# Five more of layer 0's modulation pairs made by TensorE

## The chip, the cores and the metric

The kernel runs on one core of a Trainium2 chip. The metric is the device time of one execution in microseconds. The core has TensorE (matmuls and their weight loads), VectorE, ScalarE, GpSimd, and SyncE, whose queue issues most of the DMAs. Each engine works through its own instructions in order, and semaphores order the engines among each other.

## The reference, cut to what matters

A diffusion backbone of two layers over 256 latent and 256 context tokens, width 1024. Each layer's token and channel mixers are modulated by six vectors, which come from a conditioning vector and a large matrix:

```python
def adaln(cvec, w, b):
    mod = jax.nn.silu(cvec) @ w + b
    return jnp.split(mod[..., None, :], 6, axis=-1)

def modulate(xn, shift, scale):
    return xn * (1 + scale) + shift
...
    for i in range(DEPTH):
        sh1, sc1, g1, sh2, sc2, g2 = adaln(c, ada_w[i], ada_b[i])
        csh1, csc1, cg1, csh2, csc2, cg2 = adaln(c_ctx, ada_w[i], ada_b[i])
        a = modulate(rms_norm(h, norm_mix_g[i]), sh1, sc1)
        ...
        h = h + g1 * y
        a = modulate(rms_norm(h, norm_ffn_g[i]), sh2, sc2)
```

Layer 0 has a short gated convolution (an input projection to three blocks of 1024, a convolution over three tokens, an output projection) and a dense SwiGLU; layer 1 has differential attention and a top-2-of-8 expert SwiGLU. All in float32.

## The kernel before, in words

**Weights.** Matrix weights come in units of 128x2048 float32 (1 MB). `Loads` issues their DMAs on SyncE's queue (line 53) into three raw tiles `rw`. `Parts.pump` splits a unit in a high part (line 88, a cast on ScalarE) and a low part (line 92, a subtraction on VectorE), in three pairs of tiles. A product is three matmuls, high by high, high by low, low by high (`mm3`, lines 199 to 201); a unit holds 16 blocks of 128x128, so 48 matmuls. Splits and loads are issued when the one that holds the tile is through.

**Modulation.** `ada_w` of a layer comes as 24 pairs: pair u holds two blocks of 128 output columns (for u below 8 the shift and the scale of one block of 128 channels; 8 to 11 are the first gate, 12 to 19 shift and scale of the channel mixer, 20 to 23 the second gate). `ada` (line 272) makes a pair on VectorE: four passes of 128x1024, one for each block and stream (line 279, `junk<-ra,cb`), each with a sum over the row. `ada_pe` (line 285) makes a pair on TensorE: 16 fp32 matmuls with weights of 128x128 from the raw tile and two columns (line 292, `st<-cT,ra`), into a PSUM tile `st`. It is a generator: the first two steps issue the matmuls of one block each and the second of them frees the raw tile; the third issues the end operations. These (`ada_end`, bias at line 266, gain at line 270) run on VectorE in both cases. Before the change pairs 0, 1 and 3 go by `ada_pe`, whose weights lie in the raw tile with their rows in the partitions.

Raw pairs are loaded by `aloads`, on SyncE's queue too. After the first pairs, which have four more tiles `rx`, two tiles `ra` serve all pairs in turn: pair u+2 is loaded when pair u has been consumed (`aloads.done`).

**Order.** It is written out by hand. At the start of the mixer, `mod(k)` modulates block k of the tokens (VectorE and ScalarE, lines 338, 339, 334), and `main(k)` issues 18 matmuls with it, for the first six output tiles; `main(0)` to `main(7)` use units 0 to 2. Between them stand the pairs 2 to 7 and the splits of units 1 and 2. Then comes the loop over j = 2 to 7: three tiles of 24 matmuls each (`mm`), behind the first and the second tile one pair each (`ada(0, 8)` to `ada(0, 19)`), and `conv(j, ...)`, which ends in `uh[j]` and `ul[j]` (lines 500 to 510). Seven PSUM banks serve the tiles. The output projection takes 96 matmuls over all eight `uh`, `ul` (units 12, 13), and `last_tiles` the rest of it, in matmuls of 256 columns, with the sums of squares (line 315) for the next norm.

Of the kernel before, what the change touches and what calls it, by code (L numbers as in the profile page):

```python
# [20 lines left out]
P = 128  # L21
D = 1024
KT = D // P
# [5 lines left out]
U = 2048  # L29
B = U // P  # L30
GROUPS = (6, 8, 8)
ADA_PE = (0, 1, 3)
NE = 8
HV = (0,)
NCH = FT // 2
# [107 lines left out]
def backbone(ctx: ExitStack, tc: tile.TileContext, i, out):  # L143
# [277 lines left out]
    ms = []  # L421
    run = ada_pe(1)
# [21 lines left out]
    def mod(k):  # L444
        modulate([(k, s, rs[s], ms[k], ah[k], al[k]) for s in range(2)])

    def main(k, between=None):
        for n, f in enumerate(first):
            mm3(f, *next(w), ah[k], al[k], k == 0, k == KT - 1)
            if n == 2 and between is not None:  # L450
                between()
# [15 lines left out]
    ms += [next(run), m4]  # L467
    mod(3)
    main(2)
    mod(4)  # L470
    ms.append(ada(0, 5))
    mod(5)
# [2 lines left out]
    loads.limit = len(units)  # L475
    loads.advance()
    main(3)
    ms.append(ada(0, 6))
    mod(6)
    ms.append(ada(0, 7))  # L480
    mod(7)
# [8 lines left out]
    with tc.tile_pool(name="sc", bufs=1, reuse_waits="tile") as pc:  # L490
        yp = [pc.tile([P, 2, T + 2], F32, name=f"yp{n}") for n in range(2)]
        for y in yp:
            V.memset(y, 0.0)
        uh = [pc.tile([P, T2], F32R, name=f"uh{k}") for k in range(KT)]
        ul = [pc.tile([P, T2], F32R, name=f"ul{k}") for k in range(KT)]

        def conv(j, cg, xv, bg):
            y = yp[j % 2]
            c = tp.tile([P, T2], F32, name="cs")
            A.copy(c, cg)  # L500
            V.tensor_tensor(out=y[:, :, 1:T + 1], in0=xv.rearrange("p (s t) -> p s t", s=2),
                            in1=c.rearrange("p (s t) -> p s t", s=2), op=OP.mult)
            t = tp.tile([P, 2, T], F32, name="ct")
            A.activation(t, y[:, :, 0:T], AF.Identity, scale=convw[:, 0, j:j + 1])
            V.scalar_tensor_tensor(t, y[:, :, 1:T + 1], convw[:, 1, j:j + 1], t, op0=OP.mult, op1=OP.add)
            V.scalar_tensor_tensor(t, y[:, :, 2:T + 2], convw[:, 2, j:j + 1], t, op0=OP.mult, op1=OP.add)
            f = t.rearrange("p s t -> p (s t)")
            V.tensor_tensor(out=f, in0=bg, in1=f, op=OP.mult)
            A.copy(uh[j], f)
            V.tensor_tensor(out=ul[j], in0=f, in1=uh[j].bitcast(F32), op=OP.subtract)  # L510

        conv(0, *first[:3])
        conv(1, *first[3:])
        for j in range(2, KT):
            ps = [bank() for _ in range(3)]
            for n, f in enumerate(ps):
                mm(f, w, ah, al)
                if n < 2:
                    mod0.append(ada(0, 8 + len(mod0)))
            conv(j, *ps)  # L520

        ps = [bank() for _ in range(4)]
        for k in range(KT):
            for f in ps:
                mm3(f, *next(w), uh[k], ul[k], k == 0, k == KT - 1)
        accs = [Squares(), Squares()]
        for m, f in enumerate(ps):
            for s in range(2):
                gated(f[:, half(s)], m, mod0[m // 2], s)
                accs[s].put(X[s][m])  # L530

        def last_tiles(n, hi, lo, gates, acc, mods):

            parts.release()
            parts.holding = True
            ms = range(4, KT)
            ws = [[next(w) for k in range(n)] for m in ms]
            parts.pump()

            def norm(s):  # L540
                rs = rstd(mean(acc[s], st()), s)
                return [(k, s, rs, mods[k], ah[k], al[k]) for k in range(KT)]

            def add(f, m, s):
                gated(f[:, :T], m, gates[m // 2], s)
                acc[s].put(X[s][m])

            fs = []
            for s in range(2):
                for m, b in zip(ms, ws):  # L550
                    f = bank()
                    mm(f[:, :T], b, hi, lo, half(s))
                    fs.append((f, m, s))
                    if s == 0:
                        add(f, m, s)
                    elif m == 4:
                        jobs = norm(0)
                        modulate(jobs[:4])
                    elif m == 5:
                        for j in fs[-2:]:  # L560
                            add(*j)
                        modulate(jobs[4:])
                    elif m == KT - 1:
                        for j in fs[-2:]:
                            add(*j)
            acc[1].sum()
            parts.give(1)
            parts.release(0)
            parts.holding = True
            return lambda: norm(1)  # L570

        then = last_tiles(KT, uh, ul, mod0, accs, mod0[4:])
# [891 lines left out]
def lay_out(a):  # L1464
    a = {k: np.asarray(v) for k, v in a.items()}
    x = np.concatenate([a["x"][0], a["ctx"][0]], 0)
    r = {"xT": np.ascontiguousarray(x.T.reshape(KT, P, 2, T).transpose(2, 1, 0, 3))}
    r["cc"] = np.concatenate([a["c"][0], a["c_ctx"]])[None]
    r["cT"] = np.ascontiguousarray(r["cc"].reshape(2, KT, P).transpose(2, 1, 0))
    pair = [g * KT + k for k in range(KT) for g in (0, 1)]  # L1470
    order = pair + list(range(16, 24)) + [24 + p for p in pair] + list(range(40, 48))

    adaT = a["ada_w"].reshape(2, D, 48, P).transpose(0, 2, 3, 1)[:, order]
    r["ada"] = np.ascontiguousarray(adaT.reshape(2, 24, 2, P, D).transpose(0, 1, 3, 2, 4)).reshape(2, 24, P, U)
    for k in ADA_PE:
        w = a["ada_w"][0].reshape(KT, P, 48, P)[:, :, [k, KT + k]]
        r["ada"][0, k] = w.transpose(1, 0, 2, 3).reshape(P, U)
    r["ada_b"] = np.ascontiguousarray(a["ada_b"].reshape(2, 48, P)[:, order].transpose(2, 0, 1))
    g = np.stack([a["norm_mix_g"][0], a["norm_ffn_g"][0], a["norm_mix_g"][1], a["norm_ffn_g"][1]])
    r["gain"] = np.ascontiguousarray(g.reshape(4, KT, P).transpose(2, 0, 1))  # L1480
    r["conv"] = np.ascontiguousarray(a["sc_conv_w"][0].reshape(3, KT, P).transpose(2, 0, 1))
    si = _tiles(a["sc_in_w"][0]).reshape(3, KT, KT, P, P)[[1, 2, 0]]
    so = _tiles(a["sc_out_w"][0])
    bl = [si[:, :2].transpose(2, 1, 0, 3, 4).reshape(-1, P, P), si[:, 2:].transpose(1, 0, 2, 3, 4).reshape(-1, P, P),
          so[:4].transpose(1, 0, 2, 3).reshape(-1, P, P), so[4:].reshape(-1, P, P)]
    w13 = np.stack([_tiles(a["ffn_w1"][0]), _tiles(a["ffn_w3"][0])], 1)
    w2 = _tiles(a["ffn_w2"][0])
    f = 0
    for n in GROUPS:
        bl += [w13[f:f + n].reshape(-1, P, P), w2[:, f:f + n].reshape(-1, P, P)]  # L1490
        f += n
    r["w0"] = _units(np.concatenate(bl))
    w = a["da_qkv_w"][0].reshape(2, 4, P, 3, 4, T).transpose(4, 0, 2, 1, 3, 5)
    qkv = np.concatenate([w[:, :, :, :, :2].reshape(4, 2, P, U), w[:, :, :, :, 2].transpose(0, 2, 1, 3, 4).reshape(4, 1, P, U)], 1)
    qkv = qkv.reshape(12, P, U)
    do = a["da_out_w"][0].reshape(4, 2, P, D).transpose(0, 2, 1, 3).reshape(4, P, U)
    r["w1"] = np.concatenate([qkv, do])
    r["qkg"] = np.concatenate([a["da_q_norm_g"][0], a["da_k_norm_g"][0]])[None]
    r["subg"] = a["da_sub_norm_g"][0][:, None]
    r["lam"] = a["da_lambda"][0].reshape(1, 256)  # L1500
    pos = np.arange(T)
    inv = np.float32(10000.0) ** (-np.arange(16, dtype=np.float32) / np.float32(16))
    ang = np.stack([(pos // 64).astype(np.float32)[:, None] * inv, (pos % 64).astype(np.float32)[:, None] * inv], 1)
    cos, sin = np.cos(ang), np.sin(ang)
    tab = np.stack([np.stack([cos, cos], 2), np.stack([-sin, sin], 2)])
    r["rope"] = np.ascontiguousarray(tab.reshape(2, 2, P, 64).transpose(2, 0, 1, 3))
    w13 = np.stack([a["moe_w1"][0], a["moe_w3"][0]], 2).reshape(NE, 2, 4, P, 2, 11, T)
    w13 = w13.transpose(0, 5, 1, 3, 2, 4, 6).reshape(NE, 11, 2, P, U)
    w2 = a["moe_w2"][0].reshape(NE, 11, 2, P, D).transpose(0, 1, 3, 2, 4).reshape(NE, 11, 1, P, U)
    r["moe"] = np.concatenate([w13, w2], 2).reshape(NE, 33, P, U)  # L1510
    r["router"] = np.ascontiguousarray(a["moe_router_w"][0].reshape(KT, P, NE).transpose(1, 0, 2))
    r["router_b"] = a["moe_router_b"][0][None]
    return r
# [14 lines left out]
```

## Time and profile before

| | us |
|---|---|
| median of 3 runs | 1590.19 (1588.73 to 1590.26) |
| profiled execution | 1590.32 |
| its span, first to last instruction | 1588.1 |
| TensorE busy (matmuls) | 1537.6 |
| VectorE busy | 1278.7 |
| ScalarE busy | 865.1 |
| line 279, all pairs made on VectorE | 181.0 (148 passes) |

All times in rows are microseconds from the span's start. A busy TensorE isn't TensorE at its peak: the granted clock (PEclk, 1.00 is 2.4 GHz, 0.50 is 1.2 GHz) says how fast it ran. Where a row has brackets, they hold the idle time of the engine ahead of the instruction and what ended it. Matmuls overlap, so the pace is read from start to start, not from the duration.

### The profile page before, as it was taken

How to read it: one execution, taken by the hardware profiler on the slowest of the kernel's cores; microseconds unless marked ns; L12 is line 12 of the kernel's file. 1: busy time of each engine (PE TensorE's matmuls, PEld its weight loads, DVE VectorE, ACT ScalarE, POOL GpSimd, SP SyncE). 2: the span in 40 equal slices, each digit the busy share in tenths (PEclk: the TensorE clock that was granted, in tenths of full speed). 3: DMA queues.
4: the chain of work that ended last, by engine and by line, in shares of the span. 5: the costliest groups of instructions: out<-in, count | busy, mean ns of one | idle time of the engine just before them, and what ended most of it. 6: DMA issues, size and time to landing. Idle time of an engine off the chain costs nothing. (4 is left out here: it accounts for less than half of the span.)

```text
span 1588.1 us, 20899 instructions
## 1 busy us (share of the span) xinstructions
PE 1537.6 (97%) x7582; PEld 1255.9 (79%) x7582; DVE 1278.7 (81%) x1880; ACT 865.1 (54%) x1248; POOL 45.0 (3%) x162
## 2 busy tenths in 40 slices
PE   8899899999999999999889999999999999999997
PEld 7687689888888888888777888877787777877785
DVE  5888887758838847666669999988999889998996
ACT  3232234322212224444657777877778786777774
POOL 0000000000000001211200000000000000000000
PEclk9899999999999999999999999999999999999999
DMA  9345542535637731422339999999999998999990
GB/s 369 111 160 186 192 160 106 186 133 186 212 107 263 267 106 54 160 80 80 133 144 349 364 338 364 347 378 414 360 359 363 382 419 344 345 370 407 395 362 29
DMA packets 55730, 400.35 MB, mean 252 GB/s; under 512 B 6450, under 2 KB 6482, under 8 KB 7106
## 3 DMA queue, kind: packets, MB, share of 16 engines
q1 hardware_dynamic: 55298, 398.50, 66.1%
q8 instruction: 61, 1.00, 0.3%
q0 software_dynamic: 320, 0.44, 0.2%
q14 instruction: 51, 0.41, 0.1%
HBM read 397.87 MB, written 1.05 MB: 251 GB/s over the span
## 5 line engine op out<-in xcount | busy, mean ns | idle before, releaser
L92 DVE TENSOR_TENSOR wl<-rw,wh 128x1024 fp32r<-128x1024 f32 (+1 forms) x208 | 315.9, 1549 | 84.1 <-ACT wh L88 83.5
L88 ACT CAST wh<-rw 128x1024 fp32r<-128x1024 f32 (+1 forms) x207 | 263.4, 1310 | 61.1 <-PE mm L200 56.4
L199 PE MATMUL mm<-ah,wh 128*128 128x512 f32 (+1 forms) x576 | 222.5, 386 | 5.4 <-ACT ah L339 4.5
L201 PE MATMUL mm<-ah,wl 128*128 128x512 f32 (+1 forms) x576 | 221.3, 384 | 5.2 <-DVE wl L92 5.0
L200 PE MATMUL mm<-al,wh 128*128 128x512 f32 (+1 forms) x576 | 221.2, 384 | 0.0
L92 DVE TENSOR_TENSOR wl<-rp,wh 128x1024 fp32r<-128x1024 f32 (+1 forms) x152 | 183.3, 1247 | 17.9 <-ACT wh L88 17.2
L279 DVE SCALAR_TENSOR_TENSOR junk<-ra,cb 128x1024 bf16<-128x1024 f32 x136 | 166.3, 1223 | 3.3
L88 ACT CAST wh<-rp 128x1024 fp32r<-128x1024 f32 (+1 forms) x152 | 155.4, 1070 | 2.5 <-PE h L1256 2.4
L1255 PE MATMUL h<-wh,xs 128*128 128x512 f32 x352 | 142.3, 404 | 0.0
L1257 PE MATMUL h<-wl,xs 128*128 128x512 f32 x352 | 138.9, 395 | 0.0
L1256 PE MATMUL h<-wh,xs 128*128 128x512 f32 x352 | 138.8, 394 | 0.0
L201 PEld LDWEIGHTS mm<-ah,wl 128*128 128x128 f32 x576 | 110.6, 192 | 27.8 <-DVE wl L92 7.2
L199 PEld LDWEIGHTS mm<-ah,wh 128*128 128x128 f32 x576 | 110.7, 192 | 27.6 <-ACT ah L339 5.6
L200 PEld LDWEIGHTS mm<-al,wh 128*128 128x128 f32 x576 | 110.7, 192 | 21.6 <-DVE al L334 0.9
L92 DVE TENSOR_TENSOR wl<-rq,wh 128x1024 fp32r<-128x1024 f32 x102 | 119.5, 1219 | 9.9 <-ACT wh L88 9.4
L92 DVE TENSOR_TENSOR wl<-ra,wh 128x1024 fp32r<-128x1024 f32 x96 | 113.0, 1218 | 6.7 <-ACT wh L88 6.1
L88 ACT CAST wh<-rq 128x1024 fp32r<-128x1024 f32 x102 | 101.2, 1049 | 2.1 <-PE h L1256 2.1
L88 ACT CAST wh<-ra 128x1024 fp32r<-128x1024 f32 x96 | 95.9, 1048 | 0.0
L1257 PE MATMUL y<-wl,hh 128*128 128x512 f32 x220 | 87.4, 397 | 1.5 <-DVE wl L92 1.4
L1255 PE MATMUL y<-wh,hh 128*128 128x512 f32 x220 | 87.1, 396 | 0.5 <-ACT hh L1294 0.5
L1256 PE MATMUL y<-wh,hl 128*128 128x512 f32 x220 | 86.9, 395 | 0.0
L199 PE MATMUL mm<-wh,ah 128*128 128x256 f32 (+1 forms) x256 | 83.2, 325 | 0.0
(332 smaller groups left out, 2982.9 us busy)
## 6 DMA issues: line engine op xcount, KB each, us to landing
rw<-moe SPq DMA_DIRECT2D x81, 1024.0 KB, 7.2
rp<-moe SPq DMA_DIRECT2D x79, 1024.0 KB, 7.3
rw<-w SPq DMA_DIRECT2D x61, 1024.0 KB, 4.9
ra<-moe SPq DMA_DIRECT2D x52, 1024.0 KB, 7.1
rq<-moe SPq DMA_DIRECT2D x52, 1024.0 KB, 7.5
ra<-ada SPq DMA_DIRECT2D x44, 1024.0 KB, 5.0
rx<-ada SPq DMA_DIRECT2D x4, 1024.0 KB, 19.5
rp<-w SPq DMA_DIRECT2D x4, 1024.0 KB, 6.4
```

The costliest lines, as they stand in the source:

```text
L88: self.nc.scalar.copy(hi[:, c0], raw[:, c0])
L92: engine.tensor_tensor(out=lo[:, c], in0=raw[:, c], in1=hi[:, c].bitcast(F32), op=OP.subtract)
L199: PE.matmul(ps, wh, xh, start=first, stop=False)
L200: PE.matmul(ps, wh, xl, start=False, stop=False)
L201: PE.matmul(ps, wl, xh, start=False, stop=last)
L279: V.scalar_tensor_tensor(junk, raw[:, a * D:(a + 1) * D], 1.0, cb[:, s], op0=OP.mult, op1=OP.mult, accum_out=m[:, a, s:s + 1])
L1255: PE.matmul(ps, xh, wh, start=first, stop=False)
L1256: PE.matmul(ps, xl, wh, start=False, stop=False)
L1257: PE.matmul(ps, xh, wl, start=False, stop=last)
```

## The change

Pairs 6, 11, 15, 17 and 19 of layer 0 are made by `ada_pe` in place of `ada`. Pair 6's matmuls are issued behind `main(2)`, ahead of `mod(4)`, its end operations where `ada(0, 6)` stood. Pairs 11, 15, 17 and 19 belong to the second tile of j = 3, 5, 6 and 7: their matmuls stand where `ada` stood, between the second and the third tile, their end operations behind `conv(j)`. The host lays these five pairs out with rows in the partitions, by the same order of columns as before.

```diff
-ADA_PE = (0, 1, 3)
+ADA_PE = (0, 1, 3, 6, 11, 15, 17, 19)
...
     main(2)
+    run = ada_pe(6)
+    next(run)
+    next(run)
     mod(4)
...
     main(3)
-    ms.append(ada(0, 6))
+    ms.append(next(run))
     mod(6)
...
             for n, f in enumerate(ps):
                 mm(f, w, ah, al)
-                if n < 2:
-                    mod0.append(ada(0, 8 + len(mod0)))
+                u = 8 + len(mod0)
+                if n < 2 and u in ADA_PE:
+                    run = ada_pe(u)
+                    next(run)
+                    next(run)
+                    mod0.append(run)
+                elif n < 2:
+                    mod0.append(ada(0, u))
             conv(j, *ps)
+            if 7 + len(mod0) in ADA_PE:
+                mod0[-1] = next(mod0[-1])
...
     for k in ADA_PE:
-        w = a["ada_w"][0].reshape(KT, P, 48, P)[:, :, [k, KT + k]]
+        w = a["ada_w"][0].reshape(KT, P, 48, P)[:, :, order[2 * k:2 * k + 2]]
```

## Rows read from the trace of the kernel before

**Rows 1.** Busy time by stretch: stretch, then busy us and instructions by engine.

```profile
core 0: us, PE busy (x) PEld busy (x) DVE busy (x) ACT busy (x) POOL busy (x), PEclk, DMA share, GB/s
60.00:80.00 20.00, 13.85 (x45) 9.70 (x44) 17.25 (x30) 5.25 (x7) 0.00 (x0) 0.83 0.46 158
...
180.00:200.00 20.00, 16.34 (x71) 12.84 (x70) 17.93 (x33) 3.64 (x4) 1.07 (x2) 1.00 0.52 182
...
260.00:600.00 340.00, 340.00 (x1574) 282.62 (x1574) 230.12 (x353) 93.10 (x94) 1.07 (x2) 1.00 0.51 180
600.00:1588.00 988.00, 960.31 (x4870) 775.71 (x4868) 838.15 (x1178) 689.46 (x1032) 39.28 (x147) 0.99 0.76 295
```

**Rows 2.** TensorE's waits, 60 to 220: total us, times, longest us.

```profile
PE mm L201 <- DVE wl L92: 7.2, 5, 1.8
PE mm L199 <- ACT ah L339: 4.5, 2, 4.3
PE mm L199 <- DVE ct L508: 1.9, 1, 1.9
PE mm L199 <- ACT uh L509: 1.6, 1, 1.6
```

**Rows 3.** Timeline of VectorE: start us, us, engine, line, operation, tiles.

```profile
62.87 1.22 DVE L279 SCALAR_TENSOR_TENSOR junk<-ra,cb 128x1024 bf16<-128x1024 f32 x1
...
67.93 0.16 DVE L266 TENSOR_TENSOR mod<-mod,adab 128x4 f32<-128x4 f32 x1
...
108.31 0.16 DVE L266 TENSOR_TENSOR mod<-mod,adab 128x4 f32<-128x4 f32 x1
...
212.29 0.69 DVE L510 TENSOR_TENSOR ul<-ct,uh 128x512 fp32r<-128x512 f32 x1 [0.68 <-ACT uh L509]
```

**Rows 4.** Timeline of TensorE around the pairs 1 and 3, 25 to 45.

```profile
25.53 3.41 PE L292 MATMUL st<-cT,ra 128*128 128x2 f32 x16
28.81 0.77 PE L199 MATMUL mm<-ah,wh 128*128 128x512 f32 x1
...
35.78 4.63 PE L292 MATMUL st<-cT,rx 128*128 128x2 f32 x32
40.27 0.77 PE L199 MATMUL mm<-ah,wh 128*128 128x512 f32 x1
...
44.69 0.55 PE L200 MATMUL mm<-al,wh 128*128 128x512 f32 x1
```

**Rows 5.** Stretches by granted clock (PEclk, third from the end), columns as rows 1.

```profile
35.80:38.00 2.20, 2.20 (x22) 2.20 (x20) 1.91 (x7) 0.65 (x2) 0.00 (x0) 1.00 1.03 428
38.50:44.50 6.00, 6.00 (x19) 5.13 (x20) 4.66 (x5) 1.55 (x1) 0.00 (x0) 0.50 0.46 143
65.50:68.50 3.00, 0.07 (x1) 0.00 (x0) 2.86 (x7) 0.00 (x0) 0.00 (x0) 1.00 0.55 232
69.00:75.50 6.50, 5.64 (x13) 4.35 (x14) 6.15 (x12) 0.81 (x2) 0.00 (x0) 0.50 0.42 153
```

**Rows 6.** Timeline of TensorE, 50 to 216.

```profile
50.76 0.39 PE L199 MATMUL mm<-ah,wh 128*128 128x512 f32 x1
...
69.86 0.80 PE L199 MATMUL mm<-ah,wh 128*128 128x512 f32 x1 [4.30 <-ACT ah L339]
...
77.25 0.49 PE L199 MATMUL mm<-ah,wh 128*128 128x512 f32 x1 [0.23 <-ACT ah L339]
...
81.75 0.39 PE L199 MATMUL mm<-ah,wh 128*128 128x512 f32 x1
...
146.79 0.39 PE L199 MATMUL mm<-ah,wh 128*128 128x512 f32 x1
...
215.67 0.28 PE L199 MATMUL mm<-uh,wh 128*128 128x256 f32 x1
```

**Rows 7.** SyncE's queue: two issues from 103.15 on; DMA issues, 60 to 220.

```profile
103.15 5.47 SPq L53 DMA_DIRECT2D ra<-ada  x2
...
ra<-ada SPq DMA_DIRECT2D x14, 1024.0 KB, 4.9
```

**Rows 8.** TensorE's waits, 216 to 260: total us, times, longest us.

```profile
PE st L320 <- DVE sq L315: 1.7, 2, 1.0
```

## The prediction, made before the changed kernel ran

> **What bounds the kernel now.** I read the table of 20 us stretches first, because the change touches only layer 0's mixer, the first 216 us. Behind it [rows 1] the reader sees TensorE at 340.00 busy of 340 us (260 to 600) and at 960 of 988 after that, so a shift of TensorE's work before 260 us reaches the end undiminished: I know of no later wait on anything that keeps its own time. Inside the mixer TensorE is not full: 13.85 of 20 us between 60 and 80 and 16.34 between 180 and 200, with VectorE at 17.25 and 17.93.
>
> Next, TensorE's waits between 60 and 220 us [rows 2]: 7.2 us for low halves of weights (L92, VectorE), 4.5 for ScalarE's output of `modulate` (itself waiting on VectorE), and 3.5 for the convolution's results (1.9 + 1.6). All go back to one queue, VectorE's, which is late. So the change attacks a real bound. The sum turns on what TensorE has to spare, and that is less than the waits suggest.
>
> **What a pair costs on each engine.** On VectorE the pair 6 starts at 62.87 and its bias add at 67.93 [rows 3]: 5.06 us that vanish. The bias add and the gain stay, reading PSUM instead. Five pairs are 25.3 us.
>
> On TensorE a pair is 32 records (16 fp32 matmuls of 128x2, two records each, each with a weight load of 128x128). Pair 3 is the only one made after TensorE had reached full speed [rows 4]. It starts at 35.78, and the next ordinary matmul at 40.27: 4.49 us. The stretches show two rates [rows 5]: 22 records in the 2.2 us from 35.8 to 38 at granted clock 1.00, 0.10 us each, so 3.2 us for 32 if the clock held. It did not: from 38.5 to 44.5 it is 0.50, the 1.2 GHz level, although TensorE was busy the whole time. The ten matmuls from 40.27 to 44.69 [rows 4] take 0.44 us each instead of 0.23, which is 2.1 us more. So a pair costs TensorE between 3.2 us (the clock stays at 2.4 GHz) and 6.6 us (4.49 + 2.1, pair 3). No row tells when in a later burst the clock will fall, or whether, so I take the middle, 4.9, and keep both ends. Four pairs at 4.9 are already 19.6 us, against 15.2 us of waits [rows 2].
>
> Here a rule speaks the other way. The Trainium skill, page "TensorE: Matmul & The Clock Gate", section "Why this matters for your kernels", ties drops in the middle of a kernel to gaps in which TensorE idles. By that rule a burst with no gap keeps the clock, a pair costs 3.2, and the result is the first rival below. The trace disagrees for the one burst it has: busy 2.20 of 2.20 and then 6.00 of 6.00, clock 1.00 and then 0.50 [rows 5].
>
> **Pair 6, moved to TensorE before `mod(4)`.** It sits between `main(2)` and `main(3)`, at 50.76 [rows 6]. With 4.9 us, the 54 matmuls of `main(3)` to `main(5)` at 0.23 (12.4) end at 68.1. Today they end at 65.6, and TensorE then waits 4.30 us for `mod(6)`; after that it runs `main(6)` at the low clock from 69 to 75.5 [rows 5, 6], 13 matmuls at 0.2 extra, 2.6 us. VectorE, rid of pair 6, does its small end operations at 62.9, after the split of unit 2, and `mod(6)` is out near 65. `mod(7)` and everything behind it on VectorE come 5.1 us earlier: `main(7)` starts at 77.25 - 5.1 = 72.1 and the loop of the short convolution at 81.75 - 5.1 = 76.6 instead of 81.75. Against 6.6 for the pair this would be 1 to 2 us less, against 3.2 it is the same, since `mod(7)` then ends last. The load of pair 8 (`done(6)`) moves on SP's queue ahead of the loads of units 3 to 5 and holds them until TensorE's burst ends near 55; they are split only behind `mod(7)`, past 72, 17 us later, against 4.9 us for a load [rows 7]. I cost that at nothing; if that cover were gone, it would be some 5 us.
>
> **Pair 11, and a wait that is new.** Two `ra` tiles serve all pairs, so pair 11's load is issued when pair 9 has been consumed by VectorE: today at 108.3 (its bias add [rows 3], and the second of the two loads [rows 7]). Nobody minds, as VectorE makes pair 10 and others first. After the change TensorE wants it. Pair 9 still lies on VectorE, and VectorE's chain from 62.9 to there is unbroken but for the 5.1 us of pair 6: it ends at 103.2, the load lands 4.9 later [rows 7], 108.1 or 108.2. TensorE reaches the burst after tiles 0 and 1 of block j=3: the loop runs at (146.79 - 81.75)/288 = 0.226 us per matmul [rows 6], so 76.6 + 72 x 0.226 + 48 x 0.226 = 103.7. It stands for 4.5 us. Its queue is in order: tile 2 of j=3, and with it `conv(3)` and all later blocks, stand behind it. A wait of nearly this length (4.30) brought the clock down (1.00 to 68.5, 0.50 from 69) [rows 5]. So this burst runs at the rate of the bursts before 28.8 us, 16 records in 3.28 us (25.53 to 28.81) [rows 4]: 6.7 for 32, and 2.0 more behind it, 8.7. Bounds: 3.2 (clock up at once) and 9.7 (6.7 + 3.0, half-speed a little longer than the 13 matmuls after 69.86).
>
> **The rest of the loop.** From 108.2 TensorE has 24 matmuls of j=3 (5.4), blocks 4 to 7 (4 x 72 x 0.226 = 65.0) and the output projection's 96 at the same pace (21.7): 200.3 without bursts. With 8.7 and 3 x 4.9 = 14.7 it ends at 223.7. VectorE no longer bounds it: `conv(7)` ends near 213 today [rows 3], 25 us less is 188 and so it waits for TensorE; of those waits [rows 2] none is left. Pairs 15, 17 and 19 are not late: 15 is loaded when VectorE has consumed pair 13; `conv(3)` can't end before tile 2 of j=3 (122.3) and its own last steps (2), then come a split (3.4 with its wait) and two pairs (10.3), so 138, and it is used at 108.2 + 8.7 + 5.4 + 16.3 + 10.8 = 149; 17 and 19 are freed by TensorE's own bursts 15 and 17, some 16 us ahead. Their end operations are placed after `conv(j)`, when the bursts are long done, and hold nobody.
>
> Today the output projection ends at 215.67 [rows 6]. 223.7 - 215.67 = +8.0. Behind it TensorE waits 1.7 us for sums of squares that a late VectorE delivers [rows 8]: between none and all of it comes back; I take 0.8. Net **+7.2 us**. The profiled execution took 1590.32 us (span 1588.1 and 2.2 around it), the median is 1590.19, so the forecast is **1597.5 us**.
>
> Bounds: cheap bursts and all of that 1.7 back, 200.3 + 4 x 3.2 - 215.67 - 1.7 = -4.3; dear ones, 200.3 + 9.7 + 3 x 6.6 - 215.67 = +14.1.
>
> **Rivals.** (1) *The clock holds through the three bursts 15, 17, 19*: each 3.2, 200.3 + 8.7 + 9.6 = 218.6, +2.9 - 0.8 = +2.1: 1592.4, no change that counts. For it: between 180 and 200 the clock stays at 1.00 through waits of up to 1.9 us each [rows 1, 2], so a short lull doesn't always bring it down. Against: pair 3. (2) *Pair 11 lands in time*, the rival on the other side: if VectorE's chain runs ahead so that the load is issued before 98.7 rather than 103.2, the wait and the cold burst go. Then 103.7 + 92.1 + 4 x 4.9 = 215.4, -0.3 - 0.8: 1589.2; with bursts of 3.2, 208.6, -7.1 - 0.8: 1582.4. For it: nothing: the chain of VectorE is dense; a stall elsewhere on TensorE would do it too, but costs the same. (3) *Every burst is dear* (6.6 each, 9.7 for pair 11): +14.1, 1604. Pair 3 is for it, but of its 32 records the first 22 ran at full clock. That VectorE stays the bound I leave out: the pairs are taken from its queue outright.
>
> **How the numbers follow.** The forecast holds 0.64; rival 1 0.16; rival 2 0.05 at 1589.2 and 0.05 at 1582.4; rival 3 0.10. A measurement of this kernel can tell about 0.2%, 3.2 us, from no change. Slower takes the forecast and rival 3, less a little of the forecast that lands under 1593.4: 0.72. Same, 1587 to 1593.4, takes rival 1, half of rival 2 and that little: 0.21. Faster: 0.07. The range leaves out rival 2's lower case and half of rival 3: 1588.5 to 1604.
>
> **What would show it.** Right: TensorE waits for the DMA of `ra` (line 292) some 4 us near 104; waits on L92, ct and uh between 147 and 216 are gone; the granted clock falls at most of the bursts; the first 128x256 matmul of the mixer starts near 224 instead of 215.7; VectorE's L279 has 20 instructions fewer. Wrong: no wait at pair 11 (then the step on the `ra` ring fails), or clock 1.00 across the bursts (then the price 4.9 is too high), or a gap in TensorE behind 260 us that takes up the shift.

## The result

| | before | after |
|---|---|---|
| median of 6 runs, us | 1590.13 | 1601.16 |
| profiled execution, its span | 1590.32, 1588.1 | 1601.12, 1599.4 |
| output projection of layer 0 ends (TensorE) | 215.67 | 227.85 |
| VectorE busy | 1278.7 | 1254.8 |

The changed kernel is slower: ratio 1.0067, 95% interval 1.0056 to 1.0077. VectorE did lose its 24 us, the 20 passes of line 279 that are gone. The mixer of layer 0 nevertheless ends 12.2 us later, and the span is 11.3 us longer; 0.9 us came back behind the mixer.

TensorE's waits of the kernel after, 60 to 270 us (total us, times, longest us), answer to [rows 2, 8]:

```profile
PE st L292 <- DMA ra<-ada: 2.4, 1, 2.4
PE mm L199 <- ACT ah L339: 2.3, 1, 2.3
PE st L320 <- DVE sq L315: 0.9, 1, 0.9
```

Nothing waits for the low halves (L92) or for the convolution any more. The new wait is the first line: pair 11's matmuls stand until their weights have landed. And yet TensorE's waits from 60 to 220 us have shrunk from 16.3 us (the 15.2 of [rows 2] and two smaller ones) to 4.7, so the sum of the waits does not explain the loss. TensorE's timeline of the kernel after shows where it is, the four bursts of the loop with the first ordinary matmul behind each, and the first matmul at which the pace is full again (answers to [rows 4, 6]):

```profile
78.15 0.40 PE L199 MATMUL mm<-ah,wh 128*128 128x512 f32 x1
...
107.92 6.99 PE L292 MATMUL st<-cT,ra 128*128 128x2 f32 x32 [2.40 <-DMA ra<-ada]
114.78 0.77 PE L199 MATMUL mm<-ah,wh 128*128 128x512 f32 x1
117.88 0.40 PE L200 MATMUL mm<-al,wh 128*128 128x512 f32 x1
...
148.95 4.08 PE L292 MATMUL st<-cT,ra 128*128 128x2 f32 x32
152.89 0.77 PE L199 MATMUL mm<-ah,wh 128*128 128x512 f32 x1
158.91 0.40 PE L201 MATMUL mm<-ah,wl 128*128 128x512 f32 x1
...
172.10 3.63 PE L292 MATMUL st<-cT,ra 128*128 128x2 f32 x32
175.58 0.56 PE L199 MATMUL mm<-ah,wh 128*128 128x512 f32 x1
179.32 0.39 PE L199 MATMUL mm<-ah,wh 128*128 128x512 f32 x1
...
193.62 4.34 PE L292 MATMUL st<-cT,ra 128*128 128x2 f32 x32
197.83 0.77 PE L199 MATMUL mm<-ah,wh 128*128 128x512 f32 x1
203.09 0.42 PE L199 MATMUL mm<-ah,wh 128*128 128x512 f32 x1
...
227.85 0.28 PE L199 MATMUL mm<-uh,wh 128*128 128x256 f32 x1
```

A burst has two prices: the time to the next ordinary matmul, and the matmuls behind it that run 0.43 us apart instead of 0.226. Pair 15: 152.89 - 148.95 = 3.94, then 14 matmuls from 152.89 to 158.91, 6.02 us where 3.16 would do, 2.86 more: 6.8 in all. In the same way pair 17: 3.48 + 1.7 = 5.2. Pair 19: 4.21 + 2.55 = 6.8. Pair 11, behind its wait: 6.86 + 1.5 = 8.4. The stretches say the same by the granted clock (PEclk, third from the end; columns as [rows 1]):

```profile
108.00:117.50 9.50, 9.50 (x39) 8.92 (x40) 8.57 (x13) 2.90 (x3) 0.00 (x0) 0.50 0.30 91
118.20:148.00 29.80, 29.80 (x133) 24.68 (x132) 24.17 (x38) 9.19 (x9) 0.00 (x0) 1.00 0.62 234
153.00:158.50 5.50, 5.50 (x14) 4.33 (x14) 2.25 (x4) 0.72 (x1) 0.00 (x0) 0.50 1.01 396
159.00:171.00 12.00, 12.00 (x55) 9.89 (x54) 7.97 (x12) 2.43 (x2) 0.00 (x0) 1.00 0.32 115
```

Between the bursts the clock is 1.00, and behind those of pairs 11 and 15, shown here, it is 0.50; behind 17 and 19 it is 0.50 too (176 to 179 and 198 to 202.8 us). TensorE is busy for the whole of both, so the busy column alone, full from 120 to 240 us, would look like a healthy engine.

### The profile page after: what moved, and what is told of

Same layout as the page of the kernel before. It is cut to its first block, busy times and chain, and to the rows that moved or that the text cites. A ratio compares the mean times of both kernels' runs of the same rounds, so it can differ in the third digit from the quotient of the medians.

```text
span 1599.4 us, 21181 instructions
## 1 busy us (share of the span) xinstructions
PE 1561.3 (98%) x7742; PEld 1282.6 (80%) x7742; DVE 1254.8 (78%) x1840; ACT 865.6 (54%) x1248; POOL 46.9 (3%) x162
## 5 line engine op out<-in xcount | busy, mean ns | idle before, releaser
L92 DVE TENSOR_TENSOR wl<-rw,wh 128x1024 fp32r<-128x1024 f32 (+1 forms) x208 | 316.1, 1549 | 92.2 <-ACT wh L88 91.6
L92 DVE TENSOR_TENSOR wl<-rp,wh 128x1024 fp32r<-128x1024 f32 (+1 forms) x152 | 183.5, 1248 | 17.8 <-ACT wh L88 17.2
L279 DVE SCALAR_TENSOR_TENSOR junk<-ra,cb 128x1024 bf16<-128x1024 f32 x116 | 141.9, 1223 | 2.7
L92 DVE TENSOR_TENSOR wl<-rq,wh 128x1024 fp32r<-128x1024 f32 x102 | 119.5, 1220 | 9.9 <-ACT wh L88 9.4
L92 DVE TENSOR_TENSOR wl<-ra,wh 128x1024 fp32r<-128x1024 f32 x96 | 113.0, 1220 | 6.7 <-ACT wh L88 5.6
```

The lines of the kernel that those rows point to most:

```text
L92: engine.tensor_tensor(out=lo[:, c], in0=raw[:, c], in1=hi[:, c].bitcast(F32), op=OP.subtract)
L279: V.scalar_tensor_tensor(junk, raw[:, a * D:(a + 1) * D], 1.0, cb[:, s], op0=OP.mult, op1=OP.mult, accum_out=m[:, a, s:s + 1])
```

## The experiments

Two theories stood after the result. One: VectorE and TensorE each have a chain through the mixer, the later one ends it, and the change overshot: TensorE's chain is now the longer, by the bursts, the clock that falls with them, and one wait on the ring of two `ra` tiles. The other: a pair on TensorE costs more than it frees wherever it stands. All runs are edits of the changed kernel. The column "mixer" below is the start of the first 128x256 matmul of the profiled execution, as 215.67 and 227.85 above: one execution each, while the medians are over 4 to 10. The ratios are to executions of the kernel before that were made alongside.

| run | pairs on TensorE besides 0, 1, 3 | mixer | median us | ratio to before, 95% |
|---|---|---|---|---|
| e1_pair6 | 6 | 210.19 | 1585.55 | 0.9969 (0.9958 to 0.9980) |
| e2_no11 | 6, 15, 17, 19 | 227.76 | 1602.19 | 1.0067 (1.0051 to 1.0084) |
| e3_spread | 6, 11, 15, 17, 19, spread | 222.98 | 1597.22 | 1.0030 (1.0014 to 1.0047) |
| e4_9_for_11 | 6, 9, 15, 17, 19 | 219.25 | 1594.19 | 1.0018 (1.0009 to 1.0028) |
| e5_6_9_11 | 6, 9, 11 | 208.44 | 1581.57 | 0.9936 (0.9917 to 0.9955) |
| e6_6_9_11s | 6, 9, 11, spread | 203.83 | 1579.20 | 0.9929 (0.9912 to 0.9945) |
| e7_9_for_11s | 6, 9, 15, 17, 19, spread | 212.26 | 1586.67 | 0.9977 (0.9968 to 0.9987) |
| e8_extra_dve | as changed, 12 passes more on VectorE | 228.20 | 1605.89 | 1.0096 (1.0079 to 1.0113) |
| e9_extra_dve64 | the same, other scratch tile | 227.32 | 1602.65 | 1.0077 (1.0057 to 1.0097) |
| e10_spare4 | as changed, an unread tile more | 226.90 | 1602.26 | 1.0082 (1.0054 to 1.0110) |

**Pair 6 alone.**

```diff
-ADA_PE = (0, 1, 3, 6, 11, 15, 17, 19)
+ADA_PE = (0, 1, 3, 6)
```

> Pair 6 alone goes to TensorE; 11, 15, 17 and 19 stay on VectorE. Theory (VectorE's queue sets the end of the mixer as long as few pairs are moved, and TensorE's burst of pair 6 lies in slack): VectorE's chain is 5.1 us shorter, the output projection ends at 215.67 - 5.1 = 210.6, the program takes about 1585 us, and waits on L92, ct and uh stay. Rival (a burst on TensorE is paid in full wherever it stands): pair 6 costs 5 us and gives back less, 1590 to 1595.

Measured: the mixer ends at 210.19 and the program takes 1585.55, both as expected. TensorE's waits on VectorE stay, the one on `uh` excepted. The largest of them:

```profile
PE mm L201 <- DVE wl L92: 6.0, 5, 1.8
```

So the part of the change that moves pair 6 is a gain of some 5 us, one pair's passes on VectorE. The other theory falls: a burst that lies in slack costs nothing here.

**All but pair 11.**

```diff
-ADA_PE = (0, 1, 3, 6, 11, 15, 17, 19)
+ADA_PE = (0, 1, 3, 6, 15, 17, 19)
```

> As the changed kernel, but pair 11 stays on VectorE (6, 15, 17, 19 on TensorE). Theory of the ring of two tiles (a pair that TensorE wants ahead of VectorE is loaded only when VectorE has consumed the pair two before it): pair 15 now waits in place of 11. VectorE has consumed pair 13 at 147.2 - 5.1 = 142.2, its load lands at 147, TensorE is there at 138, waits some 9 us, and the output projection ends at 147 + 8.4 + 5.4 + 32.5 + 21.7 + 2 x 6.5 = 228, as in the changed kernel: 1601 us although one burst is gone. Rival (each burst is simply paid, 11 with its wait): 10.8 us less, 1590 us.

Measured: one burst fewer and nothing won, 1602.19. The timeline has the new wait where it was expected, of 8.76 instead of 9 us, in front of a burst that runs at the low clock throughout:

```profile
146.68 6.99 PE L292 MATMUL st<-cT,ra 128*128 128x2 f32 x32 [8.76 <-DMA ra<-ada]
```

The ring holds whichever pair TensorE wants first ahead of VectorE.

**The same bursts, spread.** Two small matmuls behind each triple of the third tile, 8 x 2 = 16, in place of 16 in a row.

```diff
-                mm(f, w, ah, al)
+                mm(f, w, ah, al, small=small)
+                small = None
...
             mm3(ps, *next(w), hi[k][:, c], lo[k][:, c], k == 0, k == len(hi) - 1)
+            for _ in range(2 if small is not None else 0):
+                next(small)
```

> As the changed kernel, but the 16 small matmuls of pairs 11, 15, 17 and 19 don't stand in one burst between the second and the third tile: two of them follow each of the eight triples of the third tile. The same instructions on each engine, another order on TensorE. Theory (what a burst costs beyond 3.5 us is the clock, which falls in or behind it): the granted clock stays at 1.00 from 120 to 220, 3.0 + 1.9 + 2.9 us come back at pairs 15, 17 and 19 and up to 3 at pair 11: 1590 to 1594 us. Rival (the cost is the weight loads and small matmuls themselves): no change, 1601 us.

Measured: 1597.22, 3.9 us less, about half of what was expected. The stretches of this run show both why it was right and why it fell short:

```profile
109.20:125.80 16.60, 16.60 (x55) 14.19 (x54) 11.66 (x19) 6.04 (x6) 0.00 (x0) 0.50 0.49 171
126.50:222.00 95.50, 95.50 (x469) 80.41 (x468) 59.23 (x87) 20.84 (x20) 1.07 (x2) 1.00 0.53 182
```

From 126.5 to the end of the mixer the clock is 1.00: pairs 15, 17 and 19 no longer bring it down. A triple with two small matmuls takes 1.14 us instead of 0.68, 3.7 for a pair against 5.2 to 6.8 in bursts. But pair 11 still waits, 3.4 us here, the clock falls right behind the wait, and it stays at 0.50 through the whole mixed tile and a little beyond, 16.6 us, against some 10 behind the wait in the changed kernel. Of the ten executions three took 1589.9 to 1592.0 us, as was expected, and seven 1596.6 to 1598.7; the profiled one is of the seven. What differs in the three is open.

**Pair 9 in place of 11.**

```diff
-ADA_PE = (0, 1, 3, 6, 11, 15, 17, 19)
+ADA_PE = (0, 1, 3, 6, 9, 15, 17, 19)
```

> As the changed kernel, but pair 9 goes to TensorE in place of pair 11 (6, 9, 15, 17, 19): the same number of bursts. Pair 9 is loaded from 70 us on, so no burst has to wait for a load. Theory (the wait on pair 11's load and the low clock behind it are part of the loss): 2.4 us of waiting and some 2 us of the dearer burst go, 1597 us, with no wait of line 292 on a DMA behind 60 us. Rival (the wait costs nothing, as TensorE would wait for VectorE later anyway): 1601 us.

Measured: 1594.19, 7 us less with as many bursts. The waits of this run, 60 to 220:

```profile
PE mm L199 <- ACT ah L339: 0.9, 1, 0.9
PE st L292 <- DMA ra<-ada: 0.2, 1, 0.2
```

The wait is gone but for 0.2 us, and with it its dear burst: by the medians 7 us where some 4 were expected. The mixer even ends 8.6 earlier, but 1.7 of that need not be the edit's. The loop starts at 76.46 in this execution and at 78.15 in the changed kernel's, behind code that is the same in both; there the wait swallowed the difference, here nothing would have.

**Fewer pairs, early ones.**

```diff
-ADA_PE = (0, 1, 3, 6, 11, 15, 17, 19)
+ADA_PE = (0, 1, 3, 6, 9, 11)
```

> Three pairs are moved, 6, 9 and 11, in bursts. Theory (two queues: VectorE's chain, 215.67 less 5.06 for each pair moved; TensorE's work, 76.6 + 97.6 + 21.7 plus the bursts of the loop; the later one ends the mixer): VectorE 200.5, TensorE 195.9 + 2 x 6.5 = 209 with the bursts as dear as they were in the changed kernel: 1590 - 6.7 - 0.8 = 1583 us. Pair 11 is loaded when TensorE has freed pair 9, before TensorE needs it: no wait on a DMA. Rival (VectorE is the only bound): 1590 - 15 = 1575 us.

Measured: 1581.57, mixer 208.44 where 209 was worked out, and TensorE waits neither on VectorE nor on a DMA between 79 and 208 us. That the sum fits so well is in part luck: the loop started 1.5 late, at 78.08 instead of 76.6, and the two bursts cost 5.2 and 5.1 instead of 6.5 each. With the same two pairs spread as above:

> As the run with pairs 6, 9 and 11, but the small matmuls of 9 and 11 follow the triples of the third tile, two each. Theory: 3.7 us for a pair (the measured price of a spread pair: a triple with two small matmuls takes 1.14 us instead of 0.68) and no fall of the clock in the loop; TensorE 195.9 + 2 x 3.7 = 203.3, VectorE 200.5: 1590 - 12.4 - 0.8 = 1577 us, the fastest of all. Rival (the clock is not what bursts cost): as in bursts, 1583 us.

Measured: 1579.20 where 1577 was expected, mixer 203.83 where 203.3 was worked out. By its median it is the fastest kernel of the study, 0.7% under before, but the intervals of e5 and e6 overlap, so their times don't show that spreading gains. The mixers of the profiled executions are 4.6 us apart, and again not all of it is the edit's, as the loop of e5 (first line) starts later than that of e6 (second line) behind the same code:

```profile
78.08 0.40 PE L199 MATMUL mm<-ah,wh 128*128 128x512 f32 x1
76.46 0.39 PE L199 MATMUL mm<-ah,wh 128*128 128x512 f32 x1
```

From there to the end of the mixer it is 130.4 against 127.4, 3.0 us for two pairs, which is what bursts of 5.2 and 5.1 against twice 3.7 come to. Stretches of e5:

```profile
80.00:120.00 40.00, 40.00 (x196) 33.93 (x195) 28.82 (x39) 11.62 (x13) 0.00 (x0) 0.91 0.57 209
120.00:200.00 80.00, 80.00 (x354) 66.12 (x354) 68.69 (x107) 18.39 (x18) 1.06 (x2) 1.00 0.52 182
```

and of e6:

```profile
80.00:120.00 40.00, 40.00 (x210) 34.09 (x209) 30.82 (x43) 13.95 (x15) 0.00 (x0) 1.00 0.55 203
120.00:200.00 80.00, 80.00 (x354) 66.11 (x353) 69.89 (x107) 19.72 (x19) 1.06 (x2) 1.00 0.54 191
```

In the stretch with the two pairs, e6 gets 210 matmuls through where e5 gets 196, at clock 1.00 against 0.91; behind it they are alike.

**Five pairs without wait and without bursts.** Pair 9 for 11, and spread.

> Five pairs, 6, 9, 15, 17 and 19, the four of the loop spread over the third tile: no wait on a load and no burst in the loop. Theory (what is left is TensorE's own work): 195.9 + 4 x 3.7 = 210.7 and VectorE at 190; -5.0 - 0.8: 1584 us, and more than with two pairs in the loop. Rival (five pairs are better than three once waits and clock are out of the way): under 1577 us.

Measured: 1586.67 where 1584 was expected, mixer 212.26 (210.7 was worked out). One wait on a load is left, 0.9 us at pair 15. Each of the three parts has now a number, by the mixer: 227.85 as changed, 219.25 without the wait at pair 11 (of this 1.7 is in doubt, as said), 212.26 without the falling clock too, 203.83 with two pairs fewer in the loop. The last step is TensorE's own work, 2 x 3.7 = 7.4 of 8.4, and the 0.9 of that wait.

**Is VectorE out of the bound?** Four passes of 128x1024 are put back behind each of the bursts 15, 17 and 19, on data that nobody needs.

```diff
                     mod0.append(run)
+                    if u > 11:
+                        for s in (0, 1, 0, 1):
+                            junk = tp.tile([P, D], BF16, name="junk")
+                            V.scalar_tensor_tensor(junk, cb[:, s], 1.0, cb[:, s], op0=OP.mult, op1=OP.mult, accum_out=spare)
```

> The changed kernel, with four passes of 128x1024 put back on VectorE behind each of the bursts 15, 17 and 19, on other data and into a scratch column: VectorE does 15 us of work that nobody uses. Theory (TensorE is the bound of the loop now, VectorE stands idle some 6 us of every 20): no change, 1600 to 1603 us. Rival (what VectorE no longer does is still worth something): up to 15 us more.

Measured: 1605.89, above the theory's range and inside the rival's, though the mixer ends at 228.20, only 0.35 later. What differs lies behind it. In 250 us of plain matmuls from 300 on, long after the extra work, TensorE gets 1079 through in this run and 1094 in the changed kernel, at clock 1.00 in both. The run had one more thing than work: `spare`, a tile of 4 bytes per partition, which can shift what is allocated behind it. Two more runs separate them: the same work with a tile of 64 bytes, and the tile of 4 bytes without the work.

```diff
-        spare = const.tile([P, 1], F32, name="spare")
+        spare = const.tile([P, 16], F32, name="spare")
```

> As the run with 15 us of unused work put back on VectorE, but the scratch column lies in a tile of 64 bytes per partition in place of one of 4 bytes. In that run the mixer ended where it did without the work (228.2 against 227.85), but TensorE's pace between 300 and 550 us, far behind the extra work, was 1079 matmuls instead of 1094. Theory (the tile of 4 bytes moved every later tile, and the pace depends on where the tiles lie; VectorE's work itself is hidden): 1094 matmuls again and 1600 to 1603 us. Rival (the extra work costs 4 to 5 us): 1605 to 1607 us.

```diff
+        spare = const.tile([P, 1], F32, name="spare")
+        V.memset(spare, 0.0)
```

> The changed kernel with one tile of 4 bytes per partition more, set to zero once and never read: no work is added but that. Theory (the place of the tiles sets the pace of the matmuls): some 1079 matmuls between 300 and 550 us and 1604 to 1607 us. Rival (a tile that nobody reads changes nothing): 1094 and 1600 to 1603 us.

The stretch of 300 to 550 us, of after, e8, e9 and e10:

```profile
300.00:550.00 250.00, 250.00 (x1094) 205.01 (x1093) 174.63 (x272) 64.11 (x58) 1.07 (x2) 1.00 0.54 190
```

```profile
300.00:550.00 250.00, 250.00 (x1079) 202.14 (x1079) 171.80 (x264) 64.39 (x58) 1.07 (x2) 1.00 0.52 185
```

```profile
300.00:550.00 250.00, 250.00 (x1087) 204.03 (x1086) 173.44 (x270) 63.65 (x57) 1.07 (x2) 1.00 0.53 188
```

```profile
300.00:550.00 250.00, 250.00 (x1080) 202.13 (x1079) 172.43 (x265) 63.10 (x57) 1.07 (x2) 1.00 0.52 185
```

e10 slows the matmuls (1080) with no work but one setting to zero, so the pace goes with the tile. That it is the places of the tiles that count is argued, as no run shows an address. How much e8 owes to the tile is read from one step at the end of layer 0, the first matmul of the sums of squares behind its SwiGLU, in after, e8 and e10:

```profile
608.31 0.59 PE L320 MATMUL st<-sq,ones 128*128 128x256 f32 x2
612.49 0.59 PE L320 MATMUL st<-sq,ones 128*128 128x256 f32 x2
611.20 0.59 PE L320 MATMUL st<-sq,ones 128*128 128x256 f32 x2
```

From the end of the mixer to there it is 380.5 us in after, 384.3 in e8 and 384.3 in e10: the tile alone costs the 3.8 us, and the work adds nothing there. Nor does TensorE wait on VectorE between 79 us and the end of the mixer in e8 or e9; that e8's mixer ends 1.3 later than e10's is less than the 1.6 by which their bursts of pair 19 differ (5.1 and 3.5). So 15 us of work on VectorE are hidden, and TensorE is the bound. e9's 1602.65 us lie within the expected 1600 to 1603; that it shows 1087 rather than 1094 was not expected. e10's median, 1602.26, is not as high as expected: in the profiled execution the mixer ended 0.95 earlier than after and the time behind layer 0 was 2.6 shorter, and single runs lay between 1599.9 and 1608.2, too wide to tell 3 us.

## Why the prediction was right, step by step

The forecast was 1597.5 us and slower; 1601.16 was measured, inside the range and 3.7 us above the forecast. It is nearer to the 1604 of the third rival, which had a chance of 0.10, so the direction and the mechanism were right and the size was not.

- **The bound moves from VectorE to TensorE.** Right: the waits on L92, ct and uh are gone, and e8 and e9 hide 15 us of VectorE's work.
- **VectorE's chain.** Right to 0.3 us: `main(7)` was to start at 72.1 (72.04, behind a wait of 2.3 for `mod(7)`), pair 9 to be consumed at 103.2 (its bias add starts at 103.10), pair 11 to be there at 108.2 (107.92). VectorE's and SyncE's rows of after; the second of the two loads is issued at 103.1 and takes 4.8:

```profile
103.10 0.17 DVE L266 TENSOR_TENSOR mod<-mod,adab 128x4 f32<-128x4 f32 x1
```

```profile
97.94 5.47 SPq L53 DMA_DIRECT2D ra<-ada  x2
```

- **The wait at pair 11.** Right in mechanism and in its end, 107.92; wrong in length, 2.4 instead of 4.5, because TensorE came later. The step that failed is the start of the loop, put at 76.6: it was 78.15, as the clock fell in `main(7)`, behind the wait of 2.3 (the matmuls from 73.68 to 76.66 stand 0.43 apart). The wait at pair 11 swallowed those 1.6 us:

```profile
72.04 0.50 PE L199 MATMUL mm<-ah,wh 128*128 128x512 f32 x1 [2.30 <-ACT ah L339]
...
73.68 0.63 PE L201 MATMUL mm<-ah,wl 128*128 128x512 f32 x1
...
76.66 0.49 PE L199 MATMUL mm<-ah,wh 128*128 128x512 f32 x1
```

- **The burst at pair 11.** 8.4 measured, 8.7 forecast (16 records in 3.28 us make 6.6 for 32, not 6.7; measured 6.86). The row that it was taken from needs care: the granted clock reads 1.00 in the kernel before up to 35 us, although the plain matmuls from 29.8 to 34.5 stand 0.43 apart, so for that stretch the pace and not the clock tells the level.
- **The price of a burst at full speed.** This is the term that was mis-sized: 4.9 each, the middle of 3.2 and 6.6, against 6.8, 5.2 and 6.8. Three bursts cost 18.8 instead of 14.7, and these 4.1 us are the difference between 223.7 and 227.85; the smaller misses cancel. Pair 3's 6.6 would have been the better value, but by luck. The price is not fixed by the code of the burst: pair 3 itself, whose code the change leaves alone, takes 4.49 us to the next matmul before and 3.49 after, with the slow matmuls behind it 6.8 and 5.2. In all runs together a burst that doesn't wait for its load costs 5.1 to 5.3 or 6.7 to 6.9 where the pace falls. In five bursts it does not, and the price is 3.5: pair 3 in e3, e4, e9 and e10, and pair 19 in e10, of which these are the stretches of the burst and of the plain matmuls behind it:

```profile
195.40:198.80 3.40, 3.40 (x33) 3.40 (x32) 2.19 (x3) 0.72 (x1) 0.00 (x0) 1.00 0.88 347
199.00:203.00 4.00, 4.00 (x18) 3.22 (x18) 0.00 (x0) 0.00 (x0) 0.00 (x0) 1.00 0.75 252
```

So one row of before could give a price and not which one would come; each kernel left one trace, so whether the price differs between executions of one kernel is not shown. The lower end was also misread: 3.2 came from 22 records in 2.2 us, but a stretch counts records too that only reach into it. A burst at full clock takes 3.49 to the next matmul.
- **Rival 1**, that the clock holds, was wrong in every burst of the changed kernel's loop, and right in one of e10's. The rule that stood behind it, in the Trainium skill, page "TensorE: Matmul & The Clock Gate", section "Why this matters for your kernels", speaks of gaps in which TensorE idles; here TensorE was busy 29.80 of 29.80 us ahead of pair 15 and 5.50 of 5.50 us behind it, at 1.00 and then at 0.50, and the measurement decides. **Rival 2**, that pair 11 lands in time, did not happen, but e4 made it happen with pair 9 and won 7 us. **Rival 3** was nearly right in its price of a burst (6.6 against 6.8, 5.2 and 6.8) and too dear at pair 11 (9.7 against 8.4).
- **Behind the mixer.** 0.8 of 1.7 us were to come back; 1.7 became 0.9, and the span grew by 0.9 less than the end of the mixer moved. No later gap took up the rest.

## What to carry to other kernels

Moving work off the bound engine pays only until the other engine's chain is as long: add up both chains for each piece moved, and stop where they cross. Here they cross between one pair, where TensorE still waits on VectorE (e1), and three, where it no longer does (e5, e6); two and four were not tried. Work of another kind on TensorE costs more than its own time: sixteen narrow matmuls in a row mostly took the clock down and then cost 5 to 7 us, mixed with wide ones 3.7. Such a price read once is one value of several: look at the same piece in more than one trace before it goes into a sum. And a piece that changes engines changes its place in the ring that feeds it: ask when its load can be issued, not only when it used to be.

## What the runs showed of the hardware that was not expected

- A busy TensorE can fall to the 1.2 GHz level: in the changed kernel behind the bursts of 16 matmuls with two columns of pairs 6, 15, 17 and 19 (0.50 from 153 to 158.5 with 5.50 of 5.50 us busy). The same burst in another run can leave it at 1.00 (pair 19 in e10). A stream mixed of wide and narrow matmuls that met the low level stayed there until behind its end, 16.6 us (e3), while the same mix at the high level kept it (1.00 from 126.5 to 222).
- The pace of plain matmuls of 512 columns can change by 1.4% with a tile that they don't use, presumably by where their own tiles then lie. One unread tile of 4 bytes per partition ahead of them took 1094 matmuls in 250 us down to 1079 and 1080 (e8, e10), one of 64 bytes to 1087 (e9); the kernels without such a tile show 1094 or 1095. Which tile or address decides was not tried.
